# Up projection as seven block products for eight, in a stage of its own, then the down projection from DRAM

## The chip, the cores and the metric

One core of a Trainium2 chip runs the whole program in one launch. The metric is device time in microseconds (us), lower is better; the time given for a kernel is the median of its runs.

## The reference

Two layers of a diffusion backbone in float32 over 1024 latent tokens and 256 context tokens, model width 1024. After the mixers and the output projection, each layer ends in a gated feed-forward network with a depthwise convolution over the tokens. What the change touches is this part:

```python
def dwconv(t, w, b, pad_l, pad_r):
    ...
def conv_ffn(t, w_up, conv_w, conv_b, w_down):
    u = dwconv(t @ w_up, conv_w, conv_b, FFN_PAD[0], FFN_PAD[1])
    g, v = jnp.split(u, 2, axis=-1)
    return (jax.nn.silu(g) * v) @ w_down
...
h = h + g1 * (mix_lat @ w_out[l])
h = h + g2 * conv_ffn(modulate(rms_norm(h, norm2_g[l]), sh2, sc2), w_up[l], ...)
```

w_up is 1024 × 5632 (a gate half g and a value half v of 2816 columns each), w_down 2816 × 1024, the convolution has three taps. Layer 0 also does it for the context tokens, layer 1 for the latent tokens alone.

## The kernel before

Activations are kept transposed: channels on the 128 partitions, tokens along the free dimension. Tokens come in chunks: A and B of 512 latent tokens, c of 256 context tokens. A product of float32 precision is three matmuls: every operand is split into a rounded high half and a low remainder (`split`, lines 82 to 87: ScalarE writes the high half, GpSimd or VectorE subtracts it for the low half), and `gemm` (line 89) adds hi·hi, hi·lo and lo·hi in one PSUM bank. A "product of 512 columns" below is one such matmul on 512 tokens with 128 × 128 weights.

The feed-forward network (`ffn`, line 993) runs over 22 row tiles of 128 of the 2816 hidden channels. For tile j, `up(j, 0)` and `up(j, 1)` multiply the gate's and the value's 128 columns of w_up with all 8 channel groups of each chunk: 2 × 24 products for A, as many for B, and in layer 0 2 × 24 of 256 columns for c. ScalarE copies the banks into two rows `fr`. `conv(j, z)` is one ScalarE step and two VectorE steps (`stt`, line 80) per half, then Silu on ScalarE, a VectorE product (line 1053) and the split of the result y. `down` (line 1071) multiplies y of tile j − 1 with its 128 rows of w_down, 3 products for each of 8 output tiles and each chunk, and `add` (VectorE, `stt`) adds every bank to h with the gate factor. Only the last two tiles share a bank. Weights come by one SyncE queue into two raw slots; the six 4 KB slots for split weights are reused in turn.

Up and down are woven: the code asks for down(j − 1) between up(j, 1) and conv(j, 1). The framework orders the instructions of each engine when the program is built, by what is ready, so the order on an engine is not quite that of the code. In layer 0, `mod_rows` (line 306) also computes layer 1's modulation on VectorE in small steps, called `fillers` and drawn out of `down`.

Ahead of it, `out_proj` (line 958) finishes h for chunk after chunk and calls `norm` (line 432), which sums squares (`stats_add`), forms the row factor, spreads it over the partitions with TensorE and writes the modulated hi and lo halves (`norm_apply`, line 407). h stays in SBUF throughout the feed-forward network, 8 tiles of 5 KB a partition.

## Time and profile before

| what | us |
|---|---|
| median of 3 runs | 3075.17 |
| lowest and highest run | 3073.88, 3076.58 |
| span of the profiled execution (first to last instruction) | 3072.4 |
| TensorE busy in it | 2926.6 |
| VectorE, ScalarE, GpSimd busy | 2160.3, 1364.4, 854.8 |

The profile gives one execution's span; what lies around its first and last instruction isn't in it, and its own time isn't given beside it. Engines are named PE (TensorE's matmuls), PEld (its weight loads, which lie beside matmuls), DVE (VectorE), ACT (ScalarE), POOL (GpSimd), SP (SyncE). A group's row gives the line of the code, the engine, the operation, what it writes and reads, how many there are, the busy time and the mean of one in ns, then the idle time before them and what ended it. A timeline row gives start, length and a run of like instructions; matmuls overlap their neighbours, so the spacing of starts is their cost. The line is often that of a helper (L74 is `mm`, L80 `stt`, L71 `act`, L85 and L87 `split`).

### The profile page before, as it was taken

The numbers are of one execution on the slowest core, as the hardware profiler recorded it, in microseconds if no ns is written. First come the engines' busy times: TensorE is split into PE (matmuls) and PEld (weight loads), VectorE is DVE, ScalarE is ACT, GpSimd is POOL, SyncE is SP. The second block draws the span as 40 slices with busy tenths as digits, with TensorE's granted clock in tenths as the row PEclk, the third lists the DMA queues.
The fourth block names the chain that finished last, engine by engine and source line by source line (L and its number), as shares of the span: only waits on it lengthen the run. The fifth ranks groups of instructions, "written<-read, shape, count | busy, mean of one in ns | idle before, by whom it ended". The sixth has DMA issues, their size and how long they took to land.

```text
span 3072.4 us, 38304 instructions
## 1 busy us (share of the span) xinstructions
PE 2926.6 (95%) x15051; PEld 2356.3 (77%) x15051; DVE 2160.3 (70%) x3076; ACT 1364.4 (44%) x2186; POOL 854.8 (28%) x518
## 2 busy tenths in 40 slices
PE   7999988999999999999999889988999999999998
PEld 4668855578888888888887668955678888888887
DVE  5676898866577778677686767897726666666656
ACT  5675477733322322222223666477824232232335
POOL 1211166542221212111111211166632222222221
PEclk8999999999999999999999899999999999999999
DMA  7413200131112122222222111200030111111111
GB/s 261 139 62 100 66 9 9 38 122 40 35 54 64 55 63 73 66 79 89 63 89 75 42 35 35 76 8 8 28 89 28 48 49 49 48 48 49 48 49 62
DMA packets 194775, 188.33 MB, mean 61 GB/s; under 512 B 12874, under 2 KB 167074, under 8 KB 194594
## 3 DMA queue, kind: packets, MB, share of 16 engines
q1 hardware_dynamic: 194594, 185.88, 19.3%
q8 instruction: 118, 1.93, 0.3%
q14 instruction: 63, 0.52, 0.1%
HBM read 167.23 MB, written 18.61 MB: 60 GB/s over the span
## 4 chain that ended last, share of the span: by engine, by line
PE 74%; DVE 15%; ACT 6%; issue 2%; DMA 1%; POOL 1%; SPq 0%; DVEq 0%; ACTq 0%; POOLq 0%
PE bank L74 73%; ACT lru L71 2%; DVE lru L80 2%; DVE mt L754 2%; ACT L71 1%; DMA mraw<-in_w_mod 1%; DVE h L80 1%; PE bank L77 1%; DVE mt L758 1%; DVE lru L514 1%; DVE a L80 1%; DVE y L847 1%; DVE R L846 1%; DVE rp L670 1%; DVE nt L80 1%
## 5 line engine op out<-in xcount | busy, mean ns | idle before, releaser
L74 PE MATMUL bank<-a,w 128*128 128x512 f32 x5760 | 1387.9, 395 | 8.2 <-ACT w L71 2.5
L74 PEld LDWEIGHTS bank<-a,w 128*128 128x128 f32 x5760 | 1077.0, 189 | 243.3 <-issue 14.4
L85 POOL TENSOR_TENSOR w<-raw,w 128x1024 fp32r<-128x1024 f32 x170 | 450.8, 2653 | 1636.0 <-ACT w L71 1612.8
L80 DVE SCALAR_TENSOR_TENSOR h<-bank,mod,h 128x512 f32<-128x512 f32 (+1 forms) x888 | 574.0, 691 | 342.4 <-PE bank L74 338.9
L74 PE MATMUL bank<-y,w 128*128 128x512 f32 (+1 forms) x2688 | 595.4, 370 | 10.8 <-DVE h L80 10.6
L74 PEld LDWEIGHTS bank<-y,w 128*128 128x128 f32 x2688 | 477.1, 189 | 110.6 <-DVE h L80 17.1
L71 ACT ACTIVATE w<-raw 128x1024 fp32r<-128x1024 f32 x180 | 190.5, 1059 | 745.0 <-PE bank L74 538.2
L80 DVE SCALAR_TENSOR_TENSOR cv<-fr,fcol,cv 128x1282 f32<-128x1282 f32 (+1 forms) x176 | 340.5, 1934 | 178.5 <-ACT cv L71 175.8
L814 POOL TENSOR_TENSOR ph<-pf,ph 128x512 fp32r<-128x512 f32 x256 | 340.1, 1351 | 306.5 <-PE bank L74 172.6
L74 PE MATMUL bank<-ph,V 128*128 128x512 f32 (+1 forms) x768 | 245.5, 416 | 7.6 <-ACT ph L71 3.8
L74 PEld LDWEIGHTS bank<-ac,w 128*128 128x128 f32 x1536 | 194.6, 191 | 12.5 <-issue 4.1
L71 ACT ACTIVATE fr<-bank 128x512 f32<-128x512 f32 (+1 forms) x220 | 119.6, 544 | 189.3 <-PE bank L74 189.3
L74 PE MATMUL bank<-w,a 128*128 128x256 f32 x1536 | 200.1, 286 | 3.2 <-ACT gq L71 3.2
L74 PE MATMUL bank<-ac,w 128*128 128x256 f32 x1536 | 201.8, 285 | 1.3 <-ACT lru L71 0.8
L74 PEld LDWEIGHTS bank<-w,a 128*128 128x128 f32 x1536 | 190.2, 191 | 11.1 <-issue 5.7
L754 DVE TENSOR_REDUCE mt<-bank 128x1 f32<-128x512 f32 (+2 forms) x336 | 168.5, 534 | 38.3 <-PE bank L74 36.0
L74 PE MATMUL bank<-Q,K 128*128 128x512 f32 (+1 forms) x512 | 171.0, 428 | 2.0 <-ACT pf L71 1.6
L74 PEld LDWEIGHTS bank<-ph,V 128*128 128x128 f32 (+1 forms) x768 | 124.6, 174 | 53.4 <-ACT ph L71 16.4
L80 DVE SCALAR_TENSOR_TENSOR macc<-mraw,cond,macc 128x256 f32<-128x256 f32 (+1 forms) x196 | 130.6, 695 | 36.7 <-DMA mraw<-in_w_mod 36.1
L71 ACT ACTIVATE pf<-bank 128x512 f32<-128x512 f32 x256 | 141.9, 592 | 28.7 <-PE bank L74 27.3
L71 ACT ACTIVATE ph<-pf 128x512 fp32r<-128x512 f32 x256 | 152.2, 628 | 0.9
L74 PE MATMUL bank<-K,Q 128*128 128x512 f32 (+2 forms) x336 | 119.6, 367 | 16.6 <-DVE mt L754 12.1
(175 smaller groups left out, 2594.3 us busy)
## 6 DMA issues: line engine op xcount, KB each, us to landing
raw<-in_w_up SPq DMA_DIRECT2D x88, 512.0 KB
raw<-in_w_down SPq DMA_DIRECT2D x44, 512.0 KB
mraw<-in_w_mod SPq DMA_DIRECT2D x80, 256.0 KB
mraw<-in_w_mod SPq DMA_DIRECT2D x32, 512.0 KB
raw<-in_w_in SPq DMA_DIRECT2D x32, 512.0 KB
raw<-in_w_out SPq DMA_DIRECT2D x16, 512.0 KB
mraw<-in_w_mod SPq DMA_DIRECT2D x64, 128.0 KB
h_spill<-h SPq DMA_DIRECT2D x8, 640.0 KB
```

Of the source, the lines that this page charges most:

```text
L71: return self.nc.scalar.activation(out, in_, func, **kw)
L74: return self.nc.tensor.matmul(out, lhsT, rhs, start=start, stop=stop)
L77: return self.nc.tensor.transpose(out, in_, self.ident[:n, :n])
L80: return (eng or self.nc.vector).scalar_tensor_tensor(out, in0, scalar, in1, op0=op0, op1=op1)
L85: self.nc.gpsimd.tensor_tensor(lo, src, hi.bitcast(F32), op=OP.subtract)
L514: scan(C, A, B, 0.0, OP.mult, OP.add)
L670: nc.vector.tensor_tensor(a, xv, bc(tab[:, :, 0], HD), op=OP.mult)
L754: nc.vector.reduce_max(mt[:, 4 * s + u:4 * s + u + 1], ps[:, :n], axis=AX.X)
L758: nc.vector.tensor_tensor(m, m, mt[:, 4 * s:4 * s + 4], op=OP.max)
L814: nc.gpsimd.tensor_tensor(pl, pf, ph.bitcast(F32), op=OP.subtract)
L846: nc.vector.reciprocal(z, z)
L847: nc.vector.tensor_tensor(y, y, R, op=OP.mult)
```

## The change

The up projection of a row tile is a product of a 2 × 2 block matrix (gate and value columns by lower and upper four channel groups) with a 2 × 2 block matrix (lower and upper channel groups by chunks A and B). In place of its eight block products, a new class `UpProj` forms seven (numbers 1 to 7 in `WHAT`), 12 matmuls each. Four use sums of weight blocks (s1 to s4, two sums on VectorE and two on GpSimd for every tile, from a second load of both column halves) and four use sums of activation blocks (t1 to t4, formed once per layer in `norm` for chunk B). Product 1 is copied from PSUM by ScalarE, the others are added by VectorE to what is there, seven adds a tile. The context chunk keeps its plain products. Weight buffers are a ring of 10 (layer 0) or 14 (layer 1) units of 4 KB.

The stage runs for all 22 tiles without down: it needs the room of h, which is spilled to DRAM first, and it writes y to a new DRAM buffer `ysp` from SyncE's queue. `out_proj` takes the chunks as c, A, B, and the first products that need no sums are issued inside chunk B's norm (`ahead`); their banks are emptied in `run`. `down_proj` then loads y and w_down again tile by tile, two tiles ahead, splits them, reloads h, and accumulates two tiles in a bank, so half as many adds go to h; the first pair goes by ScalarE into separate buffers, which VectorE (A) and GpSimd (B, c) add to h. The SBUF regions are laid out in another order, with X0 and R0 ahead of H0. The modulation steps are drawn by `run`, eight a tile.

```diff
+class UpProj:
...
+        self.units = [b.W0 + 4096 * (i - 4) for i in range(10)]
+        if not self.cs:
+            self.units += [S(4) + 4096 * i for i in range(4)]
...
+    def norm(self, ch):
+        b, nc, l = self.b, self.b.nc, self.l
+        ahead = self.ahead() if ch == "B" else iter(())
+        for k in range(KT):
+            b.stats_add(ch, k)
+        next(ahead, None)
+        y = b.stats_fin(ch)
+        next(ahead, None)
+        if ch == "c":
+            return b.norm_apply(l, 1, ch, self.xc, y)
+        c0, n = CHUNKS[ch]
+        bc = b.rstd_rows(ch, y)
+        for _ in ahead:
+            pass
+        sh = lambda k: b.mod[l][:, 3, 0, k:k + 1]
+        def scaled(t, k):
+            b.stt(t, b.h[k][:, c0:c0 + n], b.gs[l][:, 1, 0, k:k + 1], bc, OP.mult, OP.mult)
+        def both(name, k, t, s):
+            hi, lo = self.x[name][k]
+            b.act(hi, t, AF.Identity, bias=s)
+            b.stt(lo, t, s, hi.bitcast(F32), OP.add, OP.subtract)
...
+        for k in range(4):
+            t1, t2, t3, t4, x2 = (f[q][k] for q in ("t1", "t2", "t3", "t4", "22"))
+            scaled(t3, k)
+            nc.vector.tensor_tensor(t1, t3, t1, op=OP.subtract)
+            scaled(x2, k + 4)
+            b.stt(t2, x2, sh(k + 4), t1, OP.add, OP.subtract)
+            b.stt(t3, x2, d[:, k:k + 1], t3, OP.add, OP.subtract)
+            b.stt(t4, t4, sh(k + 4), t2, OP.add, OP.subtract)
+            both("22", k, x2, sh(k + 4))
+            for t in ("t2", "t3", "t4", "t1"):
+                hi, lo = self.x[t][k]
+                b.split(hi, lo, f[t][k], pool_lo=t in ("t1", "t4"))
...
+    def plain(self, j, z):
+        k0 = 0 if z == 0 or self.cs else 4
+        o = self.unit()
+        oh = self.unit() if k0 == 0 else o + 2048
+        raw = self.load(j, z, k0, 8, o)
+        hi, lo = self.pair(8 - k0, o, oh)
+        self.b.split(hi, lo, raw, pool_lo=True)
+        for k in range(k0 // 4, 2):
+            q = 4 * k - k0
+            self.w[j, "gv"[z] + str(k + 1)] = hi[:, q:q + 4], lo[:, q:q + 4]
+    def sums_g(self, j):
+        o = self.unit()
+        self.sg = self.load(j, 0, 0, 8, o), o, self.unit()
+    def sums_v(self, j):
+        b, nc = self.b, self.b.nc
+        o = self.unit()
+        v, oh = self.load(j, 1, 0, 8, o), self.unit()
+        g, og, ogh = self.sg
+        tt = lambda e, out, x, y, op: e.tensor_tensor(out, x, y, op=op)
+        tt(nc.vector, v[:, 4:], v[:, :4], v[:, 4:], OP.add)
+        tt(nc.gpsimd, v[:, :4], g[:, :4], v[:, :4], OP.subtract)
+        tt(nc.vector, g[:, :4], v[:, 4:], g[:, :4], OP.subtract)
+        tt(nc.gpsimd, g[:, 4:], g[:, 4:], g[:, :4], OP.subtract)
+        for raw, r, h, names in ((g, og, ogh, ("s2", "s4")), (v, o, oh, ("s3", "s1"))):
+            hi, lo = self.pair(8, r, h)
+            b.split(hi, lo, raw, pool_lo=True)
+            for q, n in enumerate(names):
+                self.w[j, n] = hi[:, 4 * q:4 * q + 4], lo[:, 4 * q:4 * q + 4]
...
+    def context(self, j, z):
+        if not self.cs:
+            return lambda: None
+        ps = self.b.bank(self.RING)[:, :256]
+        self.b.gemm(ps, [((wh[:, k], wl[:, k]), self.xc[4 * q + k])
+                         for q in range(2) for wh, wl in (self.w[j, "gv"[z] + str(q + 1)],) for k in range(4)])
+        return lambda: self.b.act(self.fr[z][:, PC:PC + 256], ps)
+    WHAT = {1: ("g1", "11"), 2: ("g2", "21"), 6: ("s2", "t2"), 3: ("s4", "22"), 7: ("s3", "t3"), 4: ("v2", "t4"),
+            5: ("s1", "t1")}
+    def part(self, j, n):
+        b, nc = self.b, self.b.nc
+        w, x = self.WHAT[n]
+        ps = b.bank(self.RING)
+        wh, wl = self.w[j, w]
+        b.gemm(ps, [((wh[:, k], wl[:, k]), self.x[x][k]) for k in range(4)])
+        gA, gB = (self.fr[0][:, PL + 512 * i:PL + 512 * i + 512] for i in range(2))
+        vA, vB = (self.fr[1][:, PL + 512 * i:PL + 512 * i + 512] for i in range(2))
+        u = self.p1[j % 2]
+        def take():
+            add = lambda out, y: nc.vector.tensor_tensor(out, ps, y, op=OP.add)
+            if n == 1:
+                b.act(u, ps)
+            elif n == 5:
+                add(gB, gB)
+                add(vB, vB)
+            else:
+                add(*{2: (gA, u), 6: (u, u), 3: (gB, u), 7: (vB, u), 4: (vA, vB)}[n])
+        return take
+    def ahead(self):
+        for j, n in ((0, 1), (1, 1), (0, 2), (1, 2)):
+            self.late.append(self.context(0, n - 1) if self.cs and j else self.part(j, n))
+            yield
...
+    def conv(self, j, z):
+        b, fc = self.b, self.b.fcol[self.l]
...
+        g = self.cv[0]
+        b.nc.vector.tensor_mul(g[:, a0:a1], g[:, a0:a1], c[:, a0:a1])
+        b.nc.sync.dma_start(b.ysp[j][:, a0 - PC:a1 - PC], g[:, a0:a1])
...
+    def run(self, fillers):
+        b = self.b
...
+        def fill(n):
+            for _ in range(n):
+                next(fillers, None)
+        n = 4 if self.cs else 3
+        for take in self.late[:n]:
+            take()
+        for j in range(NH):
+            if j == 1:
+                for take in self.late[n:]:
+                    take()
+            if j > (0 if self.cs else 1):
+                self.part(j, 1)()
+                self.context(j, 0)()
+                self.part(j, 2)()
+            if j:
+                self.plain(j, 1)
+            if (self.cs or j) and j < NH - 1:
+                self.plain(j + 1, 0)
+            if j == 0:
+                self.sums_g(0)
+                self.sums_v(0)
+            if j < NH - 1:
+                self.sums_g(j + 1)
+            fill(2)
+            self.part(j, 6)()
+            self.part(j, 3)()
+            if 0 < j < NH - 1:
+                self.sums_v(j + 1)
+            fill(2)
+            self.part(j, 7)()
+            self.part(j, 4)()
+            if j == 0:
+                self.sums_v(1)
+            else:
+                self.context(j, 1)()
+            fill(2)
+            self.part(j, 5)()
+            fill(2)
+            self.conv(j, 0)
+            self.conv(j, 1)
...
+        chunks = [ch for ch in ("c", "A", "B") if ch in chunks]
...
+        for n in range(5):
+            spill(n)
+        up = UpProj(self, l, chunks)
+        self.T0, self.TN = self.X0 + 40960, 2
         for ch in chunks:
             for n in range(5, 8):
                 one(n, ch, ws[n - 5])
+            if ch == "A":
+                up.early()
+            up.norm(ch)
+        for n in range(5, 8):
+            spill(n)
+        self.T0, self.TN = self.X0 + 30944, 3
+        return up
...
+    def down_proj(self, l, chunks):
...
+        wspots = (A + 49152, A + 57344, X + 20608, X + 28800, X + 36992, self.W0)
+        ys, ws, accs = {}, {}, {}
+        def fetch(j):
+            o = X + 10304 * (j - 20) if j >= 20 else A + 10304 * (j % 4)
+            yh, yl = (self.sb("y", [P, PAD], F32R, o + 5152 * q) for q in range(2))
+            raw = self.sb("yr", [P, PAD], F32, o + 5152)
+            nc.sync.dma_start(raw[:, a0:a1], self.ysp[j][:, a0 - PC:a1 - PC])
+            o = A + 65536 + 8192 * (j - 20) if j >= 20 else wspots[j % 6]
+            wh, wl = (self.sb("w", [P, D], F32R, o + 4096 * q) for q in range(2))
+            wr = self.sb("wr", [P, D], F32, o + 4096)
+            nc.sync.dma_start(wr, io["w_down"][l][j * P:(j + 1) * P, :])
+            self.split(wh, wl, wr, pool_lo=True)
+            self.split(yh[:, a0:a1], yl[:, a0:a1], raw[:, a0:a1])
+            ys[j], ws[j] = (yh, yl), (wh, wl)
...
+        def group(js, parts, ring, evac):
             for ch in parts:
+                c0, m = CHUNKS[ch]
+                g = self.mod[l][:, 5, 1 if ch == "c" else 0]
                 for n in range(KT):
+                    ps = self.bank(ring[ch] if isinstance(ring, dict) else ring)[:, :m]
                     self.gemm(ps, [term(j, n, ch) for j in js])
+                    evac(n, ch, ps, g[:, n:n + 1], self.h[n][:, c0:c0 + m])
+                yield ch
+        def first(n, ch, ps, g, hv):
+            self.act(acc(n, ch), ps, AF.Copy, scale=g)
+        def add(n, ch, ps, g, hv):
+            self.stt(hv, ps, g, hv, OP.mult, OP.add)
+        order = ("A", "B", "c") if cs else ("A", "B")
+        fetch(0)
+        fetch(1)
+        self.h = self.htiles()
+        for q in range(0, NH - 2, 2):
+            fetch(q + 2)
+            fetch(q + 3)
+            if q == 0:
+                for ch in order:
+                    c0, m = CHUNKS[ch]
+                    for k in range(KT):
+                        nc.sync.dma_start(self.h[k][:, c0:c0 + m], self.hsp[k][:, c0:c0 + m])
+            for ch in group((q, q + 1), order, (0, 1, 2, 3, 4, 5, 6), first if q == 0 else add):
+                if q:
+                    continue
+                c0, m = CHUNKS[ch]
+                for n in range(KT):
+                    hv = self.h[n][:, c0:c0 + m]
+                    eng = nc.vector if ch == "A" else nc.gpsimd
+                    eng.tensor_tensor(hv, hv, acc(n, ch), op=OP.add)
+        def last(after):
+            ring = {ch: (3, 7) if ch == "c" else (0, 1, 2, 3, 7) for ch in CHUNKS}
+            for ch in group((NH - 2, NH - 1), order if cs else ("A", "B0", "B1"), ring, add):
+                after(ch)
+        return last
...
-            x = self.out_proj(l, mix, chunks)
+            up = self.out_proj(l, mix, chunks)
             fill = self.mod_rows(l + 1, range(6), 512, (self.MS0, self.rope_at + 2048)) if need else iter(())
-            last = self.ffn(l, x, chunks, fill)
+            up.run(fill)
             for _ in fill:
                 pass
+            last = self.down_proj(l, chunks)
```

## Rows read from the trace of the kernel before

**Rows 1.** The page's busy time of each engine over the span.

```profile
PE 2926.6 (95%) x15051; PEld 2356.3 (77%) x15051; DVE 2160.3 (70%) x3076; ACT 1364.4 (44%) x2186; POOL 854.8 (28%) x518
```

**Rows 2.** Busy by stretch: PE, PEld, DVE, ACT, POOL (count), PEclk, DMA, GB/s.

```profile
780.00:1640.00 860.00, 860.00 (x4596) 730.02 (x4595) 614.15 (x807) 241.79 (x273) 161.86 (x61) 1.00 0.22 66
...
2335.00:3015.00 680.00, 680.00 (x2984) 559.84 (x2984) 426.44 (x439) 210.95 (x241) 166.43 (x63) 1.00 0.16 48
```

**Rows 3.** Groups by line, 2396.9 to 2955.3 us, layer 1: busy us, mean ns.

```profile
L80 DVE SCALAR_TENSOR_TENSOR cv<-fr,fcol,cv 128x1024 f32<-128x1024 f32 x68 | 129.7, 1907 | 77.5 <-ACT cv L71 76.3
...
L71 ACT ACTIVATE cv<-fr,fcol 128x1024 f32<-128x1024 f32 x34 | 42.4, 1247 | 1.1
...
L1053 DVE TENSOR_TENSOR cv<-cv,cv 128x1024 f32<-128x1024 f32 x17 | 20.8, 1226 | 0.6
...
L71 ACT ACTIVATE y<-cv 128x1024 fp32r<-128x1024 f32 x17 | 18.0, 1060 | 96.7 <-DVE cv L1053 96.7
```

**Rows 4.** Timeline, TensorE in layer 0: start us, us, what.

```profile
1120.86 0.40 PE L74 MATMUL bank<-a,w 128*128 128x512 f32 x1
...
1121.09 1.55 PE L74 MATMUL bank<-y,w 128*128 128x512 f32 x6
...
1149.86 3.04 PE L74 MATMUL bank<-ac,w 128*128 128x256 f32 x24
...
1152.73 9.14 PE L74 MATMUL bank<-y,w 128*128 128x512 f32 x39
```

**Rows 5.** Single tiles and line 85: duration ns min/median/max.

```profile
L80 DVE SCALAR_TENSOR_TENSOR h<-bank,mod,h x824: 469/750/754, 813.6 to 2971.5; 128x512 f32<-128x512 f32 x132, 128x256 f32<-128x256 f32 x33
...
L80 DVE SCALAR_TENSOR_TENSOR cv<-fr,fcol,cv x176: 1272/1554/3753, 777.8 to 3019.9; 128x1282 f32<-128x1282 f32 x88, 128x1024 f32<-128x1024 f32 x88
...
L85 POOL TENSOR_TENSOR w<-raw,w x170: 2376/2414/7721, 43.8 to 3015.8; 128x1024 fp32r<-128x1024 f32 x170
```

**Rows 6.** Timeline, end of the output projection and chunk B's norm, layer 1.

```profile
2323.34 0.75 DVE L80 SCALAR_TENSOR_TENSOR h<-bank,mod,h 128x512 f32<-128x512 f32 x1
...
2329.75 2.06 DVE L80 SCALAR_TENSOR_TENSOR nt<-h,gs,bank 128x512 f32<-128x512 f32 x3 [0.81 <-PE bank L77]
...
2333.38 1.30 POOL L422 TENSOR_TENSOR a<-nt,a 128x512 fp32r<-128x512 f32 x1 [9.84 <-ACT a L71]
...
2334.74 10.50 PE L74 MATMUL bank<-a,w 128*128 128x512 f32 x45 [0.26 <-POOL a L422]
```

**Rows 7.** Timeline, GpSimd's split beside VectorE's convolution, layer 0.

```profile
1129.86 2.58 POOL L85 TENSOR_TENSOR w<-raw,w 128x1024 fp32r<-128x1024 f32 x1 [15.99 <-ACT w L71]
...
1130.10 3.69 DVE L80 SCALAR_TENSOR_TENSOR cv<-fr,fcol,cv 128x1282 f32<-128x1282 f32 x1
...
1134.11 1.55 DVE L80 SCALAR_TENSOR_TENSOR cv<-fr,fcol,cv 128x1282 f32<-128x1282 f32 x1
```

**Rows 8.** Groups by line, window 845.1 to 1612.8 us, layer 0.

```profile
L80 DVE SCALAR_TENSOR_TENSOR cv<-fr,fcol,cv 128x1282 f32<-128x1282 f32 x74 | 150.4, 2033 | 35.5 <-ACT cv L71 34.7
...
L80 DVE SCALAR_TENSOR_TENSOR macc<-mraw,cond,macc 128x256 f32<-128x256 f32 x98 | 49.6, 543 | 11.6 <-DMA mraw<-in_w_mod 11.4
L80 DVE SCALAR_TENSOR_TENSOR macc<-mraw,cond,macc 128x512 f32<-128x512 f32 x56 | 47.8, 853 | 8.0 <-DMA mraw<-in_w_mod 7.7
...
L1053 DVE TENSOR_TENSOR cv<-cv,cv 128x1282 f32<-128x1282 f32 x18 | 26.8, 1489 | 0.3
...
L332 DVE TENSOR_SCALAR macc<-mraw,cond 128x256 f32<-128x256 f32 x14 | 7.4, 562 | 0.0
```

**Rows 9.** The page's line of what the DMA engines moved, by slice.

```profile
GB/s 261 139 62 100 66 9 9 38 122 40 35 54 64 55 63 73 66 79 89 63 89 75 42 35 35 76 8 8 28 89 28 48 49 49 48 48 49 48 49 62
```

**Rows 10.** Timeline, TensorE at the end of the down products, both layers.

```profile
1656.15 1.65 PE L74 MATMUL bank<-y,w 128*128 128x512 f32 x6 [1.09 <-DVE h L80]
1659.06 3.92 PE L74 MATMUL bank<-y,w 128*128 128x512 f32 x18 [1.25 <-DVE h L80]
...
3029.43 9.94 PE L74 MATMUL bank<-y,w 128*128 128x512 f32 x42 [0.96 <-DVE h L80]
```

More of the change, by code (lines that the diff above doesn't have):

```diff
@@ L405, in stats_fin, with rstd_rows @@
         return y
+    def rstd_rows(self, ch, y):
+        n = CHUNKS[ch][1]
+        bc = self.bank((4, 5))
+        for b in range(n // P):
+            self.tr(bc[:, b * P:(b + 1) * P], y[:, b:b + 1].to_broadcast([P, P]))
+        return bc
     def norm_apply(self, l, w, ch, x, y):
@@ L410, in norm_apply @@
         c = 1 if ch == "c" else 0
-        bc = self.bank((4, 5))
-        for b in range(n // P):
-            self.tr(bc[:, b * P:(b + 1) * P], y[:, b:b + 1].to_broadcast([P, P]))
+        bc = self.rstd_rows(ch, y)
         for k in range(KT):
@@ L975, in out_proj @@
             if n == 0 and l == 0:
-                rows = self.mod_rows(l, (4,), 1024, [self.MS0] + [self.X0 + 24576 + 2048 * q for q in range(3)])
+                rows = self.mod_rows(l, (4,), 1024, [self.MS0] + [self.X0 + 2048 * q for q in range(3)])
             for ch in chunks:
@@ L1136, in build @@
         assert self.rc.at <= self.rc.size, self.rc.at
-        self.T0 = self.X0 + 30944
+        self.T0, self.TN = self.X0 + 30944, 3
         self.params_early()
```

178 lines of the change are left out of this document (82 added, 96 removed).

## The prediction

> **What bounds the kernel now.** I read the page's busy times first, then busy time by stage, then the feed-forward stretches by instruction group, then single collisions and the stage edges. Over the span TensorE is busy 95%, VectorE 70%, GpSimd 28% [rows 1]. By stage the feed-forward network is TensorE without a gap: 860 of 860 us in layer 0 and 680 of 680 us in layer 1, at a granted clock of 1.00, which is the 2.4 GHz level [rows 2]. So a removed matmul counts in full, as long as every other engine keeps up.
>
> What a matmul costs: in the layer-1 window of 558.4 us, 17 row tiles pass (17 tensor_mul of line 1053 [rows 3]), 32.85 us each. A tile takes 2 × 48 up and 48 down products of 512 columns, 144, back to back; so 0.228 us each. A context product of 256 columns: 24 of them separate the start of one run from the next by 152.73 − 149.86 = 2.87 us, 0.12 each [rows 4]. The layer-0 window of 767.6 us holds 18 tiles, 42.6 us each; 144 × 0.228 + 72 × 0.12 = 41.5, and the rest, about 0.9, is the modulation work woven in.
>
> **The products.** Per row tile and layer, up goes from 96 to 84 products of 512 columns, 12 × 0.228 = 2.74 us; 22 tiles, 2 layers: 120 us. Context products and down products stay. Up alone takes 96 × 0.228 = 21.9 us a tile in layer 1 and 21.9 + 5.8 + 0.9 = 28.6 in layer 0; after the change TensorE needs 19.2 and 25.8.
>
> **What has to keep up.** Down no longer lies between two up tiles, so VectorE and GpSimd do a tile's convolution in 19 to 26 us rather than 33 to 43, with more to do. VectorE per tile, layer 1: four convolution steps of 1.27 (shortest, [rows 5]), the gate product 1.23 [rows 3], two weight sums of 512 columns at 0.69 (the three nt of 2.06 in [rows 6]), together 7.7; and seven adds out of PSUM at 0.75 (priced as the h add, [rows 5]), 5.3; total 13.0. Layer 0: 4 × 1.55 [rows 7], 1.49 [rows 8], 1.4, and modulation: 49.6 + 47.8 + 7.4 = 105 us in 18 tiles [rows 8], some 12 of it blocked (below); as 15 of its 16 column groups lie there, 4.5 a tile over 22 tiles; together 13.6, with the adds 18.9. GpSimd: low halves of 1024 columns at 2.41 (median, [rows 5]), four a tile in layer 0, three and a half-size one at 1.30 in layer 1, and two weight sums at 1.30 (size of the one in [rows 6]): 12.2 and 11.1, against 3 × 2.41 = 7.2 a tile before.
>
> These two engines exclude each other on some work. A convolution step that takes 1.55 us alone took 3.69 when it began 0.24 us after a GpSimd split of 2.58 us [rows 7]: it waited the split out. Over the kernel these steps run from 1.27 to 3.75, while the h add, with one operand in PSUM, has median 0.75 and maximum 0.75 [rows 5]. So VectorE work with both operands in SBUF and GpSimd work share one thing: 13.6 + 12.2 = 25.8 us a tile in layer 0 and 7.7 + 11.1 = 18.8 in layer 1, against TensorE's 25.8 and 19.2. That is a load of about 100%. Adds out of PSUM can run under GpSimd; if none did, VectorE and GpSimd in a row would take 31.1 and 24.1. These are the ends of the tile's time.
>
> The Trainium skill (SBUF — State Buffer, Who interferes with whom) says the same as an exclusive lock held for the whole instruction, with VectorE instructions of at most one SBUF input exempt; the trace agrees (0.75 against 0.75). By that rule alone the sum would rest on the 25.8 and 18.8 just found, and the products' saving would be nearly whole.
>
> Which value I take: in the windows of before the steps cost 2.03 rather than 1.55 us in layer 0, 74 in 18 tiles, and the modulation (543 and 853 ns [rows 8], against h adds of its sizes at 469 and 750 [rows 5]) another 0.7 a tile: 2.7 us blocked, 37% of GpSimd's 7.2. In layer 1, 1.91 rather than 1.27, four times a tile: 2.5 us, 35% [rows 3, 8]. VectorE worked on SBUF pairs for 34% and 23% of a tile then (with the y split, which has the size of the gate product), and for about 52% and 39% after the change; scaled with that, 57% and 59% of GpSimd's time block VectorE, 6.9 and 6.6 us. VectorE comes to 25.8 and 19.6, TensorE's own time. One wait comes on top: the convolution starts only after the last product's two adds and ScalarE's first step, 1.25 us in layer 1 [rows 3] and by its columns some 1.5 in layer 0, in which GpSimd can go on; I count half. A tile then takes 26.5 us in layer 0 (saves 2.1) and 20.2 in layer 1 (saves 1.7): 22 × 3.8 = 84 us.
>
> **Entering the stage.** Before, chunk B's norm was hidden: the next up products of chunk A ran meanwhile, and TensorE idled 0.26 us before it took B up [rows 6]. Five of the seven products now need chunk B's norm, so only four groups (layer 1: 4 × 12 × 0.228 = 10.9 us; layer 0: two groups and two context groups, 11.2) can run ahead. From the last h update at 2323.34 to the first norm instruction was 6.4 us [rows 6]. Then VectorE does nine instructions of 0.69 for each of four k, 25 us, of which the last needed second operand is near the end: 30 us, and GpSimd's eight splits of 1.30 block some of that, 4. TensorE has 10.9 + 6.2 (three groups' first three k) + 1.6 of small work by then: 15 us idle in layer 1. In layer 0 the weight sums of tile 0 lie in the old h tiles, free at about 28 us; 1 MB at the fastest slice's 261 GB/s [rows 9] is 4 us, the sums and splits 0.7 + 1.3 + 0.7 + 1.3 + 1.3 + 2.4 more, 40 us in all with blocking; TensorE has 11.2 + 5.6 (tile 1) + 2.8 + 1.6: about 20 idle. Ends: 8 and 25 each.
>
> **Leaving it.** Down starts with loads and splits of y and w_down; their places free up after tile 21's first and third products, 11 us before its last. All ready in time: 0. All behind the last convolution on VectorE and ScalarE (1.5 + 1.5 + 3.1 + 1.3 + 3.1 + 1.5, then the split 1.3 + 1.5, by the sizes of [rows 8]): 15. No row decides; I take the middle, 8 in each layer.
>
> **Down.** Products unchanged: 22 us a pair in layer 1 and 28 in layer 0, for 2.1 to 2.3 MB, 100 GB/s against 261 in the fastest slice. VectorE has 16 to 24 adds (12 to 16 us) and two splits, GpSimd two splits: covered; if loads come late, seven banks give 7 × 6 × 0.228 = 9.6 us of cover. Half the adds go, and so does VectorE's hold on TensorE at the stage's end, 1.09 + 1.25 in layer 0 and 0.96 in layer 1 [rows 10]: minus 3. The h and y round trips lie beside products: nothing, and if their cover is gone 2 MB at 261 GB/s, 8 us a layer. ScalarE does four high halves a tile, of the convolution step's 1024 columns and so near its 1.25 [rows 3], two such steps at up to 1.5 and a few smaller ones, some 11 of 20 us: nothing.
>
> **Sum.** −84 + 15 + 20 + 16 − 3 = −36 us. The span is 3072.4; the median of the runs is 2.8 higher, which I add as what lies around it: 3075.2 − 36 = 3039 us.
>
> **Rivals.** First, TensorE stays the bound: GpSimd works a tile ahead, since its buffers hold one tile more, and the shared load just fits. Tiles at 25.8 and 19.2, the whole −120, with the same edges of +48 −72: 3003 us; with the entries at 8 each and nothing at the exits (16 − 3 in all) 2968. The Trainium skill (Perfetto Trace Analysis, Identifying the Most-Contended Engine) points here, as it goes by the engine of highest occupancy; the 95% of [rows 1] bear it out for the kernel before, not for one with a shared lock at 100%.
>
> Second, slower: VectorE and GpSimd take turns. Place: the convolution of tile j, blocked by the splits of tile j + 1, holds the seven PSUM banks. Halfway to doing everything in a row, tiles take 28.5 and 21.6: −2 and −7, edges +48: +39, 3114 us. From a mean loss of (120 − 48) / 44 = 1.6 us a tile against TensorE's own time it decides the sign. For it: the load of 100%. Against it: PSUM banks and weight buffers let both sides run a tile apart.
>
> Third, also slower: the y store sits on SyncE's queue ahead of the next second-half weights. If SyncE waits for the gate product (about 16 us into a tile in layer 0) and only then loads (0.5 MB, 2 us) for the split (1.3 + 2.4), the weights come at 22 us, and TensorE has 16.5 us of other products first: some 5 us a tile, and 4 by the smaller sizes of layer 1. That is 22 × 9 = 198 against the −72 of the first rival: about 3201. Against it: the built order is not the code's order; up products stand among down products [rows 4], so the queues were ordered by readiness.
>
> **Numbers.** Forecast 0.45, TensorE the bound 0.25, turns 0.22, queue 0.08. Time 3039; with entries at 8 to 25 and exits at 0 to 15 each, the forecast alone runs from 3004 to 3068. The range takes in the first rival and the turns: 2985 to 3114. This kernel's measurement can tell about 0.2%, 6 us, from no change. Faster: forecast and first rival, less 0.02: 0.68. Same: 0.08, where forecast and turns meet. Slower 0.24.
>
> **What would show it.** Right: in the up stage 84 products a tile, tiles spaced near 26.5 and 20.2 us, convolution steps with means well above 1.6, TensorE idle 15 to 20 us on VectorE or GpSimd as each layer's stage begins, under 10 as it ends. Wrong: TensorE idle on PSUM adds in every tile (turns); SyncE waiting long on the gate product (queue); no idle at all between tiles (first rival).

## The result, and the profile after

The changed kernel takes 3117.43 us (median of 4 runs, 3116.54 to 3120.11), the kernel before 3074.53 beside it: ratio 1.0142, 95% interval 1.0127 to 1.0156. It is 43 us slower; the forecast was 36 us faster. The profiled execution's span is 3118.3 us against 3072.4.

The page's busy times, which answer to [rows 1]:

```profile
PE 2859.0 (92%) x14523; PEld 2283.4 (73%) x14523; DVE 2289.3 (73%) x3098; ACT 1398.5 (45%) x2198; POOL 1228.1 (39%) x726
```

528 matmuls are gone (44 tiles x 12), but TensorE's busy time fell by 68 us, not by the 120 that they are worth at 0.228 us: many of those left run longer. The stages show where. Busy by stretch as in [rows 2] (PE, PEld, DVE, ACT, POOL with counts, granted clock, DMA share, GB/s), in order: entry, up and down of layer 0, then the same of layer 1:

```profile
761.00:839.00 78.00, 56.27 (x255) 44.04 (x254) 71.12 (x87) 28.12 (x39) 36.21 (x26) 0.82 0.30 94
839.00:1453.00 614.00, 541.12 (x2877) 456.34 (x2877) 482.11 (x488) 187.68 (x204) 270.53 (x120) 0.93 0.45 133
1453.00:1791.00 338.00, 328.76 (x1654) 276.12 (x1655) 227.15 (x316) 87.60 (x108) 87.65 (x47) 0.98 0.29 103
2396.00:2455.00 59.00, 43.09 (x142) 28.23 (x141) 51.30 (x61) 23.78 (x34) 30.89 (x23) 0.80 0.23 72
2455.00:2846.00 391.00, 390.93 (x1723) 323.25 (x1723) 283.49 (x292) 160.71 (x166) 243.13 (x121) 1.00 0.43 130
2846.00:3106.00 260.00, 254.83 (x1167) 208.33 (x1166) 169.98 (x225) 76.98 (x111) 62.55 (x32) 0.99 0.27 96
```

Layer 1's up is what was hoped for, TensorE without a gap at a clock of 1.00. In layer 0's up it idles 73 of 614 us, and the mean granted clock is 0.93, so a part of the time was spent at the lower of its two levels, 1.2 GHz. From the first update of h in layer 0's output projection to the last down product of layer 0 the changed kernel takes 80 us more than before; from there to the first update of h in layer 1, which stands behind its attention, 9 less; the rest 27 less.

The groups of layer 0's up, 839 to 1453 us, in which 20 gate products (VectorE's product of the two halves, line 240, one a tile) pass, 30.7 us apart (answer to [rows 8]):

```profile
L316 DVE SCALAR_TENSOR_TENSOR cv<-fr,fcol,cv 128x1282 f32<-128x1282 f32 x80 | 172.6, 2216 | 34.9 <-ACT cv L307 34.9
...
L316 DVE SCALAR_TENSOR_TENSOR macc<-mraw,cond,macc 128x256 f32<-128x256 f32 (+1 forms) x140 | 134.2, 981 | 28.8 <-DMA mraw<-in_w_mod 28.1
...
L240 DVE TENSOR_TENSOR cv<-cv,cv 128x1282 f32<-128x1282 f32 x20 | 30.3, 1514 | 1.6 <-ACT cv L307 1.5
```

Their counterparts in layer 1, 2512.8 to 2856 us, 18 tiles (answer to [rows 3]; the last row is the first of VectorE's two weight sums of a tile, from the view by form):

```profile
L321 POOL TENSOR_TENSOR w<-wr,w 128x1024 fp32r<-128x1024 f32 x72 | 173.5, 2431 | 115.7 <-ACT w L307 107.6 <-PE bank L310 8.0
...
L316 DVE SCALAR_TENSOR_TENSOR cv<-fr,fcol,cv 128x1024 f32<-128x1024 f32 x72 | 105.5, 1523 | 15.7 <-ACT cv L307 15.7
...
L168 DVE TENSOR_TENSOR wr<-wr 128x512 f32<-128x512 f32 x17 | 23.3, 1369 | 0.0
```

A convolution step of layer 1 costs 1.52 us, nearer to the 1.27 of one alone [rows 5] than to the 1.91 of before [rows 3], although GpSimd has half as much work again (11.1 us a tile for 7.2, as priced in the prediction). In layer 0 a convolution step costs 2.22 us, 2.03 before, and a modulation step 0.98 instead of 0.54 to 0.85 [rows 8]. The waits in the layer-0 window 886.8 to 1439.6 us (waiting engine, line, what was waited for: us in all, times, longest; SPq is SyncE's DMA queue):

```profile
PE bank L313 <- DVE ms L583: 67.5, 10, 11.0
...
DVE cv L316 <- ACT cv L307: 32.6, 10, 6.7
DVE macc L316 <- DMA mraw<-in_w_mod: 28.1, 28, 2.4
DVE wr L168 <- DMA wr<-in_w_up: 21.8, 16, 3.8
...
SPq L555 <- DVE macc L316: 125.7, 87, 5.4
SPq L241 <- DVE cv L240: 104.9, 13, 11.1
```

Three in-order queues are standing. TensorE's holds the modulation's transposes (line 313) until VectorE has copied their input; SyncE's holds the modulation's loads (line 555), which have two buffers, until VectorE has used one up, and the y stores (line 241) until the gate product is done; VectorE in turn waits for ScalarE and for loads that come late. After such a stop TensorE can also be slower. Its timeline after one of 8.61 us (start us, duration, idle before):

```profile
1040.31 0.69 PE L313 MATMUL bank<-ident,ms 128*128 128x128 f32 x2 [8.61 <-DVE ms L583]
1040.65 8.20 PE L310 MATMUL bank<-xt,w 128*128 128x512 f32 x24
1048.68 3.04 PE L310 MATMUL bank<-ac,w 128*128 128x256 f32 x24
1051.55 2.91 PE L310 MATMUL bank<-xt,w 128*128 128x512 f32 x12
1054.30 2.88 PE L310 MATMUL bank<-x,w 128*128 128x512 f32 x12
```

From start to start, the first 24 matmuls take 8.03 us, 0.33 each; the twelve from 1051.55 on take 2.75, 0.23 each, the price of a product at a granted clock of 1.00.

### The profile page after: what moved, and what is told of

It reads as the page before. It is cut to its first block, busy times and chain, and to the rows that moved or that the text cites. A ratio compares the mean times of both kernels' runs of the same rounds, so it can differ in the third digit from the quotient of the medians.

```text
span 3118.3 us, 38974 instructions
## 1 busy us (share of the span) xinstructions
PE 2859.0 (92%) x14523; PEld 2283.4 (73%) x14523; DVE 2289.3 (73%) x3098; ACT 1398.5 (45%) x2198; POOL 1228.1 (39%) x726
## 4 chain that ended last, share of the span: by engine, by line
PE 52%; DVE 25%; DMA 8%; ACT 7%; issue 5%; POOL 2%; SPq 0%; DVEq 0%; ACTq 0%; POOLq 0%
PE bank L310 51%; DVE cv L316 4%; DMA wr<-in_w_up 3%; DMA mraw<-in_w_mod 3%; ACT lru L307 2%; DVE macc L316 2%; DVE lru L316 2%; DVE mt L994 2%; PE bank L313 1%; ACT cv L307 1%; ACT L307 1%; DVE fr L208 1%; DVE mt L998 1%; DVE xt L323 1%; DVE y L1087 1%
## 5 line engine op out<-in xcount | busy, mean ns | idle before, releaser
L321 POOL TENSOR_TENSOR w<-wr,w 128x1024 fp32r<-128x1024 f32 (+1 forms) x220 | 560.6, 2567 | 518.6 <-ACT w L307 467.4
L310 PE MATMUL bank<-xt,w 128*128 128x512 f32 x2112 | 530.7, 405 | 37.2 <-POOL w L321 10.6
L310 PEld LDWEIGHTS bank<-xt,w 128*128 128x128 f32 x2112 | 408.2, 196 | 136.0 <-POOL w L321 14.5
L307 ACT ACTIVATE w<-wr 128x1024 fp32r<-128x1024 f32 (+1 forms) x220 | 223.4, 1018 | 548.3 <-POOL wr L168 377.7
L316 DVE SCALAR_TENSOR_TENSOR h<-bank,mod,h 128x512 f32<-128x512 f32 (+1 forms) x448 | 302.9, 687 | 200.3 <-PE bank L310 199.6
L310 PE MATMUL bank<-a,w 128*128 128x512 f32 x1536 | 388.8, 405 | 9.9 <-ACT a L307 2.4
L310 PE MATMUL bank<-x,w 128*128 128x512 f32 x1584 | 394.3, 400 | 2.5 <-DVE fr L208 1.7
L310 PEld LDWEIGHTS bank<-x,w 128*128 128x128 f32 x1584 | 303.7, 194 | 68.6 <-DVE fr L208 2.6
L310 PEld LDWEIGHTS bank<-a,w 128*128 128x128 f32 x1536 | 287.5, 191 | 85.7 <-issue 11.7
L321 POOL TENSOR_TENSOR w<-raw,w 128x1024 fp32r<-128x1024 f32 x38 | 102.0, 2685 | 422.7 <-ACT w L307 422.7
```

Of the source, the lines that this page charges most:

```text
L307: return self.nc.scalar.activation(out, in_, func, **kw)
L310: return self.nc.tensor.matmul(out, lhsT, rhs, start=start, stop=stop)
L316: return (eng or self.nc.vector).scalar_tensor_tensor(out, in0, scalar, in1, op0=op0, op1=op1)
L321: self.nc.gpsimd.tensor_tensor(lo, src, hi.bitcast(F32), op=OP.subtract)
```

## The experiments

Theories: **queue** (work that waits in an in-order queue in front of work that is needed) and **turns** (VectorE and GpSimd are full, as their exclusion makes them). e7, e12, e13, e14 and e16 leave out a part of layer 1's modulation and serve only to price it. The table has all kernels; "L0" and "L1" are the mean distance of the gate products 3 to 21 in each layer's up, "down" is layer 0's down stage, first to last product, all in us of the profiled execution, the ratio is to before.

```
kernel                 median    ratio   95% interval       L0    L1    down
changed                3117.43   1.0142  1.0127 to 1.0156   30.7  18.9  338
e1  mod in down        3103.96   1.0103  1.0081 to 1.0124   27.4  19.0  389
e2  late transposes    3135.85   1.0199  1.0184 to 1.0214   31.8  19.0  331
e3  more GpSimd        3194.02   1.0391  1.0368 to 1.0415   27.4  23.3  392
e4  eight products     3123.17   1.0161  1.0144 to 1.0178   27.6  21.5  383
e5  e1, store on ACT   3052.45   0.9923  0.9906 to 0.9941   24.7  19.0  381
e6  e1, 8 buffers      3081.49   1.0019  1.0009 to 1.0029   27.2  18.9  377
e7  no mod on TensorE  3127.35   1.0165  1.0150 to 1.0180   30.6  18.9  338
e8  e5 and e6          3043.69   0.9888  0.9873 to 0.9903   24.8  19.1  379
e9  store on ACT       3104.40   1.0087  1.0070 to 1.0103   29.7  19.1  337
e11 mod shared         3045.73   0.9904  0.9888 to 0.9919   26.5  19.0  349
e12 e9, no mod loads   3064.42   0.9955  0.9939 to 0.9972   27.9  19.1  338
e13 e9, short steps    3093.49   1.0058  1.0043 to 1.0073   29.6  19.0  340
e14 e9 and e7          3109.21   1.0108  1.0093 to 1.0123   29.2  19.1  334
e15 e8, later ones     3030.85   0.9851  0.9836 to 0.9866   24.8  19.1  367
e16 e12 and e7         3055.96   0.9940  0.9924 to 0.9957   25.8  19.1  335
e17 e9, loads on POOL  3121.55   1.0156  1.0141 to 1.0171   30.6  19.1  335
e18 e9, 4 buffers      3097.01   1.0067  1.0051 to 1.0084   29.5  19.1  338
```

**e1: the modulation of layer 1 is drawn in down, not in up.**

```diff
+                    if n in (1, 4, 7):
+                        next(fillers, None)
+                        next(fillers, None)
...
-            up.run(fill)
+            up.run(iter(()))
+            last = self.down_proj(l, chunks, fill)
```

> The modulation steps of layer 1 are drawn in the down stage (six for each chunk of eight banks) instead of the up stage; nothing else changes. Theory Q (queue): in the changed kernel TensorE idles because the small modulation transposes stand in its queue and wait for a VectorE copy that is behind blocked convolution steps, and the clock falls after each such wait. Then layer 0's tiles go from 30 us to 26 to 27, the granted clock of that stretch from 0.93 to 0.98 or more, and the time to about 3030 us. Theory T (turns): VectorE and GpSimd exclude each other and the tile is as long as their turns. Then only the 4.5 us of modulation a tile and what it blocks leave VectorE, TensorE still idles on adds and weights in every tile, tiles are 28 us or more, and the time is 3070 us or more.

The tile fell to 27.4 us, still 2.7 above the 24.7 of e5, where TensorE has no gap, and down took 51 us more. The time is where turns had it, the tile between the two theories. In up, TensorE now waited for weight sums, and the chain behind them, in the window 883.3 to 1375.8 us, leads to the y store: once per tile SyncE stands at it for 13.5 us, the next load behind it is late, VectorE waits for that.

```profile
PE bank L310 <- POOL w L321: 34.1, 17, 2.8
...
DVE wr L168 <- DMA wr<-in_w_up: 81.1, 18, 5.4
...
SPq L241 <- DVE cv L240: 243.4, 18, 15.2
```

**e2: the transposes six draws after the copy instead of one**, with 12 draws a tile for 8.

```diff
-            yield
+            for _ in range(6 if l else 1):
+                yield
```

> As the changed kernel, but each modulation group's transposes are drawn six steps after their copy rather than one, and twelve steps are drawn a tile rather than eight; VectorE, GpSimd and TensorE have the same work in the same stage. Theory Q: TensorE's waits for that copy (71 us in twelve waits) nearly vanish and with them the low clock, layer 0's tiles take 26 to 27.5 us, the time is 3030 to 3055 us. Theory T: the load is the same, so tiles stay near 30 us and the time within 10 us of 3117.

The wait for the copy went, and 81.9 us (13 times) of waiting for VectorE's modulation sums came in its place, one step earlier in the same chain: small matmuls with ones take these sums, and the copy and the transposes come behind them. The time rose by 18 us, which neither theory had. The run tells that TensorE's wait follows VectorE's delay, not who delays VectorE.

**e3: e1, with four more GpSimd subtractions of 512 columns a tile in layer 1.**

```diff
+        if not self.cs:
+            ms = b.sb("ex", [P, 4, P], F32, b.MS0)
+            for _ in range(4):
+                nc.gpsimd.tensor_tensor(ms, v[:, :4], v[:, 4:], op=OP.subtract)
```

> As e1, with four more GpSimd subtractions of 512 columns a tile in layer 1's up stage, written to a place nothing reads: 4 x 1.30 = 5.2 us more a tile, GpSimd at 16.3 us, GpSimd and VectorE's work on SBUF pairs together at 24.0 us against TensorE's 19.2. Theory T: the tile grows to 24 us, 22 x 5 = 110 us more than e1. Theory Q, with turns no bound: the tile stays within 1 us of e1's (19.0 in the changed kernel), at most 20 us more.

Layer 1's tile is 23.3 us: the two engines' times add up, and a tile of 19.0, TensorE's own time there, becomes one of 23.3. The groups of VectorE in layer 1 of e3, 2519.5 to 2939.1 us:

```profile
L320 DVE SCALAR_TENSOR_TENSOR cv<-fr,fcol,cv 128x1024 f32<-128x1024 f32 x72 | 175.7, 2498 | 30.1 <-ACT cv L311 30.1
L168 DVE TENSOR_TENSOR wr<-wr 128x512 f32<-128x512 f32 x17 | 38.8, 2284 | 0.0
L212 DVE TENSOR_TENSOR fr<-bank,p 128x512 f32<-128x512 f32 x54 | 36.7, 679 | 0.0
```

Work on SBUF pairs grew (2498 ns against 1523; a sum of 2284 against 0.69 us alone), the add with an operand in PSUM did not (679 ns, 682 in the changed kernel). So the exclusion is real; the load that the change leaves in layer 1 just fits under TensorE's 19.0.

**e4: e1 with 96 plain products** (the stage of its own stays).

> As e1, but all eight block products, as 96 plain products a tile with ScalarE copying the banks; no sums of weights or activations, one load of each weight half. The stage of its own, the spill of h and the DRAM round trip of y stay. Both theories: TensorE needs 21.9 us a tile in layer 1 and 27.7 in layer 0. If the seven products give all they take away, tiles are 2.7 us longer than e1's, 120 us in all, less some 20 to 40 us of idle at the two entries that need no sums: e1 plus 80 to 100 us. If e1's tiles are held by anything else in layer 0, the difference is smaller there.

By the table the seven products give 21.5 − 19.0 = 2.5 us a tile in layer 1; in its steady tiles (21.8 apart; the first distance counted, 17.6, is short) 2.8, as counted. In layer 0 they give 0.2, as what they free is lost to e1's waits: e4's TensorE has no gap there, and beside e5, which has none either, it is 27.6 − 24.7 = 2.9. The time is only 19 us above e1's, not 80 to 100: e4's first gate product of layer 0 comes 10 us sooner after the last update of h, and the rest was not followed up.

**e5, e6, e8: e1 with the y store on ScalarE's queue, with eight buffers for the modulation's loads, with both.**

```diff
-        b.nc.sync.dma_start(b.ysp[j][:, a0 - PC:a1 - PC], g[:, a0:a1])
+        b.nc.scalar.dma_start(b.ysp[j][:, a0 - PC:a1 - PC], g[:, a0:a1])
...
-            fill = self.mod_rows(l + 1, range(6), 512, (self.MS0, self.rope_at + 2048)) if need else iter(())
+            fill = self.mod_rows(l + 1, range(6), 512, [self.W0 + 8192 + 2048 * i for i in range(8)]) if need else iter(())
```

> The kernel of e1 (modulation drawn in down), with the y store alone issued from ScalarE's queue instead of SyncE's, so that the next sums' value half is no longer behind a wait for the gate product. If the stall of 52.8 us on the sums in layer 0's up stage comes from that load (queue), the tile of layer 0 falls from 27.4 to 25.2-25.5 us (TensorE alone 24.9), layer 1 stays at 19.0, and the time is 40 to 50 us below e1's 3104: 3055 to 3065. If the sums come late because VectorE and GpSimd exclude each other there (turns), the tile stays at about 27.4 and the time at about 3104. If ScalarE's own steps are held behind the store's wait, the tile gets longer than 27.4.

> The kernel of e1, with eight buffers instead of two for the rows of the modulation weights that down of layer 0 draws. If the 389 us of layer 0's down in e1 (338 in the changed kernel) are waits of the ones products on loads, down falls to 335-345 and the time to 3055-3060. If they are the price of the modulation's small matmuls on TensorE wherever they stand, down stays at 380 or more and the time within 10 us of 3104. Layer 0's up tile stays at 27.4 in both.

> The kernel of e1 with both edits, the store on ScalarE's queue and eight buffers in down. If both waits are what is lost (queue), tile 25.3 us in layer 0, down of layer 0 about 335 us, time 3000 to 3015: faster than the kernel before. If turns rule layer 0's up stage, the tile stays at 27.4 and the time at about 3055.

e5 settles the store: 51 us, and layer 0's up is TensorE without a gap, at a clock of 1.00 (18 tiles, 880.4 to 1324.9 us of e5):

```profile
880.40:1324.90 444.50, 444.50 (x2366) 385.23 (x2365) 294.48 (x254) 165.64 (x181) 232.50 (x107) 1.00 0.37 115
```

e6 met neither number: 22 us, 12 of them in down. TensorE's waits for the modulation's sums in down were 21.8 us in e1 and 23.6 in e6, so the buffers were not their cause. e8 is faster than before by 1.1%, but 29 to 44 us above what was expected: down took 379, not 335.

**e7: the changed kernel without the TensorE part of layer 1's modulation.**

```diff
+            if l:
+                yield
+                yield
+                yield
...
+                    nc.vector.tensor_copy(m, pc[:, O_BM + 8 * j + n0:O_BM + 8 * j + n0 + w // P])
...
+                continue
```

> The changed kernel, with the TensorE part of the modulation of layer 1 left out (the products with ones, the copy and the transposes; layer 1's modulation is the bias alone), so a part of the computation is missing; the modulation's VectorE products and its loads stay. If TensorE's in-order queue, with transposes that wait for VectorE's copy, makes layer 0 slow (queue), its tile falls from 30.7 to 26.5-28 us, the clock rises to 0.97 or more and the time falls by 60 to 80 us to 3037-3057. If VectorE and GpSimd are simply full there (turns), the modulation's VectorE work is still there: tile about 30, time within 15 us of 3117.

No gain: 3127. The transposes, with the longest of TensorE's waits in that stage, are where it stood, not the reason. Without them it waited for weights instead (49 us for GpSimd's splits, 22 for ScalarE's, in 18 tiles).

**e9, e11: the store's edit of e5 alone, on the changed kernel; and with half of the modulation in each stage.**

> The changed kernel with one edit: the y store is issued from ScalarE's queue, and the modulation stays in the up stage. If the store's place on SyncE's queue is what makes layer 0 slow, the modulation's own load can be borne: tile of layer 0 from 30.7 to 25.8 (TensorE with the modulation) to 26.5 us (the forecast), 22 x 4.2 to 4.9 = 92 to 108 us less: 3010 to 3025. If VectorE's load with the modulation holds the tile (turns), it stays at 28.5 or more and the time at 3070 or more.

> The store on ScalarE's queue, and the modulation spread evenly over both stages of layer 0: one draw where the changed kernel has two in up, and one draw where e5 has two in down, with two buffers. If what is lost with the modulation is the rate at which its loads and TensorE steps come, both stages get shorter than where one holds it all: up's tile about 25.3 us, down of layer 0 340 to 350 (e5 380, e8 379), time 3010 to 3025, below e8's 3044. If each step costs the same wherever it stands, the time is within 10 us of e8's or e5's.

e9 fell short by 79 to 94 us: with the modulation in the stage, moving the store gives 1.0 us a tile, not 2.7. e11's tile and time (26.5, 3046) also miss: sharing is worth no more than e8. The modulation still costs 5 us a tile in e9, whose SyncE stands at the modulation's loads, with the up weights behind them (window 886.8 to 1421.9 us):

```profile
SPq L555 <- DVE macc L316: 172.2, 87, 9.8
SPq L141 <- PE bank L310: 106.8, 25, 8.7
```

**e12, e13, e14: e9 without the modulation's loads, with little of its VectorE time, without its TensorE part.**

```diff
+            if l and i >= len(bufs):
+                raws[i] = keep[i % len(bufs)][:, :w]
+                return
...
-                    self.stt(acc[c], raw, col, acc[c], OP.mult, OP.add)
+                    n = 32 if l else w
+                    self.stt(acc[c][:, :n], raw[:, :n], col, acc[c][:, :n], OP.mult, OP.add)
```

> The kernel of e9 (changed kernel, store on ScalarE's queue; tile of layer 0 29.7 us) with the loads of layer 1's modulation weights left out but for the first two, so VectorE multiplies the same two blocks again and again: that modulation is not the reference's, and its VectorE and TensorE work is all there. If the loads, which wait on SyncE's queue for VectorE (181 us in e9's up stage) with the up weights behind them, hold the tile (queue): 27 us or less, about 60 us below e9, near 3045. If VectorE's time holds it (turns), or the transposes in TensorE's queue: 29 or more, time within 15 us of 3104.

> The kernel of e9 with seven of every eight modulation steps of layer 1 on VectorE cut to 32 columns (the other columns' terms are left out); the loads, the waits of the queues and TensorE's part stay. VectorE loses some 3.5 of its 24 us a tile. If VectorE's time holds the tile (turns): 27 us or less, near 3045. If SyncE's queue or the transposes do: 28.5 or more, 3080 or above.

> The kernel of e9 with the TensorE part of layer 1's modulation left out, as in e7 (the modulation is the bias alone). If the transposes in TensorE's queue hold the tile when the store no longer does: 27 us or less, near 3045. If VectorE's time or the loads do: 29 or more in the tiles that have modulation steps, time within 15 us of 3104.

e12 gave 40 us, more than either other: 27.9 a tile, and SyncE now waits almost only for free weight places, so it runs ahead again. What went is VectorE's own waiting for loads, 35.2 us in e9's 18 tiles and 4.3 in e12's, 1.7 a tile:

```profile
DVE macc L316 <- DMA mraw<-in_w_mod: 30.6, 27, 3.0
DVE wr L168 <- DMA wr<-in_w_up: 4.6, 8, 1.0
```
```profile
DVE wr L168 <- DMA wr<-in_w_up: 4.3, 7, 2.0
```

The modulation's traffic as such is not seen to slow the up weights: VectorE waits 4.6 us for them with it and 4.3 without. In e13 VectorE is busy 2.6 us a tile less than in e9 (384.79 for 431.15 in 18 tiles) and the tile stays. The waits and the busy time of e13 (18 tiles, 875.7 to 1409 us) show VectorE waiting for the loads in the time it was given:

```profile
875.70:1409.00 533.30, 478.59 (x2553) 403.24 (x2552) 384.79 (x449) 165.62 (x182) 237.47 (x107) 0.95 0.46 136
```
```profile
DVE macc L316 <- DMA mraw<-in_w_mod: 53.2, 30, 4.8
...
SPq L555 <- DVE macc L316: 217.0, 75, 14.7
```

e14 gave nothing, as e7. There the modulation steps, no longer held by TensorE's part, all come early: 33 to 36 us a tile while they last, 23 to 27 after.

**e16, e17, e18: e12 and e14 together; e9 with the loads on GpSimd's queue; e9 with four buffers for the first half of the loads.**

```diff
-            nc.sync.dma_start(raws[i], self.io["w_mod"][l]
+            (nc.gpsimd if l else nc.sync).dma_start(raws[i], self.io["w_mod"][l]
...
+            four = [o + 1024 * i for o in (self.MS0, self.rope_at + 2048) for i in range(2)]
+            fill = chain(self.mod_rows(l + 1, range(2), 512, four),
+                         self.mod_rows(l + 1, range(2, 6), 512, four[::2])) if need else iter(())
```

> The kernel of e12 (the modulation's loads left out but for two; 27.9 us a tile) with the TensorE part of layer 1's modulation left out too, as in e14; only the modulation's VectorE work is left. If that work, some 4.5 us a tile, is borne by the stage (queue), TensorE is the bound: 24.7 to 25.3 us a tile, 55 to 70 us below e12, 2995 to 3010. If VectorE and GpSimd are full with it (turns): 27 or more, 3045 or above.

> The kernel of e9 with layer 1's modulation loads issued from GpSimd's queue instead of SyncE's; nothing is left out. If the up weights' place behind these loads is what cost (queue), the tile falls from 29.7 to about e12's 27.9 and the time to 3065, as long as GpSimd, which now waits for VectorE before each such load, isn't itself held. If GpSimd's splits are held as SyncE's loads were, the tile stays at 29 or gets longer, and the time stays at or above 3104.

> The kernel of e9 (29.7 us a tile) with the two buffers of the modulation loads cut into four for the loads of 256 columns, which are the first half; the second half has two as before. If the loads cost because each is issued only after VectorE has freed one of two buffers and VectorE then waits for it (34 us in e9's up stage, 60 in e17's, none in e12's), the first half's tiles fall to about 28, those of the second half stay near 30, and the time falls by 15 to 25 us to 3080-3090. If the number of buffers decides nothing, both halves stay at 30 and the time within 8 us of 3104.

e16: the modulation's VectorE work, all that is left, comes in the first tiles. Of the distances one is 29 us, three are 34 to 35 and one is 27; then it costs none. That is 25.8 by the table's measure, which leaves out the first two, and 26.4 over all 21 (e12 27.5, changed kernel 30.1, e5 24.5). The time, 3056, missed 2995 to 3010 and lies where turns had it; it is only 8 us below e12. In the three long tiles VectorE is as good as full, 98.77 of 103.2 us:

```profile
877.70:980.90 103.20, 85.90 (x399) 70.24 (x398) 98.77 (x94) 27.37 (x30) 43.29 (x18) 0.90 0.26 81
```

e17: SyncE runs ahead, but GpSimd stands at the loads instead (178 us in 845 to 1390 us), its splits behind them, and the tile is no better. e18: VectorE's wait for the modulation's loads shrank (3.8 us in the half with four buffers, 12.6 in the other; 15.8 and 18.4 in e9), and the tiles stayed at 29 to 30 in both halves. In the 18 tiles the wait moved to the up weights behind those loads, 15.9 and 16.0 us for e9's 30.6 and 4.6:

```profile
DVE wr L169 <- DMA wr<-in_w_up: 16.0, 11, 4.8
DVE macc L317 <- DMA mraw<-in_w_mod: 15.9, 18, 2.5
```

So it is neither the number of buffers nor SyncE as such: in whichever of the two in-order queues the loads stand, they wait there for VectorE, and the stage's own work waits behind them. A queue with nothing else in it was not tried.

**e15: e8, with the modulation in down drawn three steps at a time, and its products with ones and its transposes drawn later.**

```diff
-            yield
-            yield
+            for _ in range(6 if l else 2):
+                yield
```

> The kernel of e8 (3044), its modulation in down drawn three steps at a time, with four more steps between the last product and the products with ones, and one more before the transposes. If down's loss there (379 us with the modulation, 338 without) is TensorE standing for sums that aren't ready (29 us in nine waits in e8), down falls to about 350 and the time to 3010 to 3020. If each step is paid for wherever it stands, down stays at 375 or more and the time at 3044.

3030.85 us, ratio 0.9851, the best of all, 44 us below before. TensorE's waits for the modulation's sums in down fell from 28.6 us in e8 to 5.6 (those for the copy rose from 1.5 to 8.4), and down by 12, not to 350; the rest, 367 against 338 without modulation, is not explained. Here a later draw helped, in e2 not; that VectorE has the slack to catch up in down and not in layer 0's up would explain it, but no run shows it.

## Why the prediction was wrong

**The products, right.** 12 matmuls of 0.228 us went per tile: 2.8 us in layer 1's steady tiles by e4 against e1 and 2.9 in layer 0 by e4 against e5, 2.74 counted; TensorE's own tile is 24.7 in e5 (forecast 25.8 with 0.9 of modulation, 24.9 without; the rest of 42.6 − 41.5 is 1.1, not 0.9) and 19.0 (19.2).

**Layer 0's tile, wrong: "A tile then takes 26.5 us in layer 0".** It took 30.7; instead of −2.1 a tile +2.1, 22 × 4.2 = 92 us, more than the whole miss of 79. The failing step is "One wait comes on top ... I count half": VectorE's own time was estimated well enough (436 us busy in 18 tiles is 24.2, forecast 25.8), but it also idled 6.5 us a tile, for which 0.7 was counted. I took the modulation for VectorE work alone; its loads, with two buffers on SyncE's queue, and its matmuls in TensorE's queue wait for VectorE, and the stage's weights and products wait behind them. Before, a tile of 42.6 us left room for that.

From the first update of h in layer 0 to its first down product the changed kernel takes 803 us. Taken away in this order, the parts are worth, in that stretch: the store 15 us (e9), the loads 39 (e12), the TensorE part 8 (e16), the VectorE work 50 (691 in e5); over 22 tiles 0.7, 1.8, 0.4 and 2.3. The stretch is that of one execution of each kernel, and a kernel's runs lie 4 to 16 us apart, so the 8 is not clear of noise. In the other order the modulation, taken first, is worth 65 us (e1) and the store 47 (e5). So the parts do not add: each wait covers another. And the largest of the four parts is VectorE's own load, which the sum had as 4.5 us in every tile; in e16, with no loads and no TensorE part to wait for, it came in a few tiles that VectorE filled.

**Layer 1's tile, also wrong, the other way: "20.2 in layer 1".** It took 19.0, a further 22 × 1.2 = 26 us. The mis-sized term is "57% and 59% of GpSimd's time block VectorE, 6.9 and 6.6 us": measured as the prediction measured it before, 72 convolution steps at 1.52 rather than 1.27 us and 17 first sums at 1.37 rather than 0.69 make 30 us in 18 tiles, 1.7 a tile for the 6.6. VectorE was busy 13.6 us a tile (245.1 in 18), where 19.6 were forecast. The share of before did not carry over. The sum by exclusion alone, 18.8, lies under TensorE's 19.2 and had layer 1 right, and e3's 23.3 lies near the 24.0 of that sum with the added work. The Trainium skill (SBUF — State Buffer, Who interferes with whom) calls the port pair that VectorE and GpSimd share an exclusive lock; layer 1 and e3 agree with it by these numbers.

**The entries, right in idle time, short of the clock.** "About 20 idle" and "15 us idle": TensorE idled 21.7 and 15.9 us. But the clock was 0.82 and 0.80 there, some 56.3 × 0.18 = 10 us and 43.1 × 0.20 = 9 us more, if all of what clock was lost was lost to work. It is an estimate; the forecast had no such term. **The exits**, 8 each: TensorE idles 8.1 us between 1453 and 1519 at a clock of 0.87 to 0.94 in layer 0, and 0.1 us from 2846 to 2880 in layer 1.

**The rivals.** "TensorE stays the bound" is what layer 1 does. "Turns" has the time, 3114 against 3117, by luck (its tiles were 28.5 and 21.6, measured 30.7 and 19.0), and a part of the cause: VectorE's modulation work alone costs 50 us (e16 against e5). It does not have the whole: e13 gives VectorE 2.6 us a tile back, and the tile stays; layer 1, where its sum was as near to full, ran at TensorE's pace. "Queue" named the mechanism, the store on SyncE's queue, and e5 shows it (2.7 us a tile, forecast 5; nothing in layer 1), but "the queues were ordered by readiness" was no argument against it: the order is fixed when the program is built, and SyncE waits at the store for the real gate product, 243.4 us in e1's 18 tiles. I weighed the rivals as exclusive cases. In layer 0 two of the queues' waits, and VectorE's load, came together.

**What stays open:** what VectorE's modulation work costs when it is spread evenly and nothing else of the modulation stands in a queue, as in every run that left out TensorE's part it came early; how much of layer 0's loss is the clock and how much the waits; and why down costs 29 us more with the modulation even in e15.

## What to carry to other kernels

When a stage is shortened, list everything that was woven into it, with every queue that each piece occupies and every wait that it makes there: work that hid in 42 us need not hide in 25. Read waits on DMA queues as on engines; a store that waits for the end of a tile belongs on a queue with nothing urgent behind it. And the engine with the longest wait (67.5 us on one line here) may be only the last to notice: take the suspected cause away before pricing it, and take pairs away. The store and the modulation, each moved alone, gave 15 and 65 us up to layer 0's first down product, and together 112; in the kernel's time it was 13, 13 and 65, as down takes 42 to 51 us more with the modulation.

## What was not expected of the hardware

Engines that exclude each other can share a tile almost without loss: 18.8 us of VectorE and GpSimd work, as priced, in tiles of 19.0, with 1.7 blocked, where the same engines in the kernel before, with two thirds of the GpSimd work, lost 2.5 a tile. And the mean granted clock was 0.93 in layer 0's up of the changed kernel, where TensorE stops for up to 11 us; in e1, whose stops are at most 2.8 us, 0.99; in e5, without any, 1.00.
